# A two-layer encoder step on one core: weight sums formed in place one chunk a pair, casts ordered by edges, adds moved between two engines

## The chip, the cores and the metric

The kernel runs on one core of a Trainium2 chip. The metric is the device time of one execution in microseconds, the median of several runs. TensorE does the matrix products, VectorE, ScalarE and GpSimd the work between them, and SyncE's queue issues nearly all transfers between the chip's memory (HBM) and the on-chip buffers (SBUF). TensorE writes its sums to PSUM banks, from which VectorE and ScalarE fetch them. Each engine works through its own instructions in order: one that waits holds up all behind it.

## The reference, cut to what matters

Two layers on 1024 prompt frames and 64 sample frames (1088 columns, `T`), model width 1024:

```python
for layer in range(DEPTH):                       # DEPTH = 2
    if layer < N_A:                              # layer 0: state-space mixer
        mp, hp_new, cp_new = ssd_mixer(rmsnorm(xp, nw[0]), h0, c0, *params)
    else:                                        # layer 1: banded attention on a shared K/V
        ...
        mp = prompt_band_attention(qp, kp, vp, attn_rel_bias[i]) @ attn_w_o[i]
    xp = xp + rmsnorm(mp, nw[1])
    xp = xp + rmsnorm(swiglu(rmsnorm(xp, nw[2]), ffn_w_in[layer], ffn_w_out[layer]), nw[3])
    ...                                          # the same for the sample frames

def swiglu(u, w_in, w_out):
    g, up = jnp.split(u @ w_in, 2, axis=-1)
    return (jax.nn.silu(g) * up) @ w_out         # hidden width 2816
```

The change lies in the feed-forward part (`swiglu`) of both layers and in what follows it in layer 0: the second normalisation, the residual, and the operands of layer 1's first products. All data are 32-bit.

## The kernel before

**Products.** A 32-bit operand is split into a high part (ScalarE casts it) and a low part (VectorE subtracts the cast from the value), and a product of two such operands takes three matmuls: high x high, high x low, low x high. A tensor of the activations is held with the model width on the partitions; the 1088 columns are four quarters, `QS`: q = 0 and 1 of 256, q = 2 and 3 of 288. Column half b = 0 is quarters 0 and 1, b = 1 is quarters 2 and 3.

**Seven products in place of eight.** Both matrices of the feed-forward part are cut into 2 x 2 blocks, and seven block products P1 to P7 (`PRODS`, `SINGLE`) with sums of blocks before and after take the place of eight. So weights appear as plain parts `r0` and `b22` and as the two sums `ta` and `tb`, and the hidden activations as blocks `a11`, `a12`, `a21`, `a22` and sums `s1` to `s4`.

**First matrix, the pair loop.** `RUN` lists 22 positions. Position 0 is hidden tile pair 5 and position 1 pair 4 (b = 1 only), positions 2 to 17 are pairs 6 to 21 (both b), positions 18 to 21 are pairs 0 to 3 (b = 1 only). (Pairs 0 to 4 of b = 0 run before it without block sums, `plain_pairs`.) `run_pair` (L1454 on) issues a pair's products in order, P1 (b=0), P1 (b=1), P2 (b=0) and so on, 14 in a pair of both halves, each of 12 matmuls (L1485 to L1487), and after each its evacuation: a ScalarE copy (L1497) or VectorE adds (`add`, L1474) and, at the end, the hidden products (`times`, L1470). P6 and P7 go on adding into the bank that P1 filled, so they wait until ScalarE's copy has read it; P3 goes on in P5's bank, after VectorE's add has read it.

**Weights** (`Weights`, L234 on). `load` (L265) brings two tiles `raw` a pair; `pair` forms `ta` and `tb` (L323, L324, L341, L342; the first two on GpSimd, or on VectorE where the item has "dve"), and `part` (L369, L370) splits `b22`, `r0`, `ta`, `tb`. The three places for split weights (`hl`) are freed as the pair's products finish, r0's after P2, and refilled for the next pair. The cast of `b22` has a gate: GpSimd copies one column of `W.last`, the pair before's cast `ta`, into its output tile (L367), so that the cast can't start before that. All this is issued with priority `W.pri`, 3000 (`HIP`) within the loop; the evacuations have 3000 too. The planner that orders VectorE, ScalarE, GpSimd and the transfers takes among the ready instructions the one first in program order, with the priority counted as so many instructions earlier. TensorE's order is that of the program.

**Late work** (`hid.late`). After each product but the first P1 of a pair, one late step is issued (two where only b = 1 runs and more than four wait). Late steps are the block sums of the hidden activations (`form`, L1358: 4 for each b, after every second pair, and put ahead of others) and the chunks of the second matrix's weight sums (`chunk`, L1412). There are 16 chunks a layer, each of four sums `WT1` to `WT4` of four blocks, which `load` (L1399) brings from HBM and whose results go back to HBM (`wt`, L1413) for the second matrix. `side` queues them after a position's products: two chunks at positions 2, 8, 10, 12, 14 and 16 (with three empty steps between them), one at 9, 11, 13 and 15, none at 3 to 7; the first blocks are loaded at position 1, those of the third chunk at 7, and the others as soon as the chunk before is formed. A chunk uses five tiles of the ring `sg` (`SGB` = 5): its four blocks and `d`. The first sum of a chunk or a block group has a gate too, a one-column VectorE copy (L1406, L1353) from `hid.gate`, the last ScalarE evacuation.

**Operand loader.** After pair 21 `loader7` brings the blocks of the hidden activations from HBM (L1735) and `late_cast` splits them (L1704, L1705); within the loop a GpSimd copy of one column of `hid.gate` (L1702) is the gate.

**Second matrix** (`wino`, L1531 on; matmuls L1583 to L1585). `PHASES`: P1, P6, P2, P7, P5, then P4 (b=0), P4 (b=1), P3 (b=0), P3 (b=1). Each evacuation adds to the accumulators `p1`, `u2`, `u3`, `c22` (L1612), and `square` sums the squares for the normalisation (`add_sq`, L520 to L525: ScalarE squares, GpSimd or VectorE adds).

**Quarter ends of layer 0** (`EndU`). A quarter is finished after P4 (q = 0, then 2) or P3 (q = 1, then 3). `rb_steps` takes the sum of squares: matmuls with ones (L532), ten small VectorE steps (L538 to L549), a diagonal (L553), a matmul that spreads it (L561), a ScalarE copy (L567, L569). Then for each of 8 column blocks m: scale (L1835), add the residual (L1836, odd m on GpSimd but for q = 3), split for layer 1 (`split`, L1792 and L1793: one ScalarE cast and one VectorE subtraction for each m and each of one or two parts), square and sum again (`tail`, on GpSimd for q < 2 and odd m). The split operands `u` lie in cells of 384 columns, three to a tile (`u_slice`). Layer 1's first products (L498 to L500) need all m of a slice: slice 0 is quarter 0 and half of quarter 1.

## Time and profile before

| | |
|---|---|
| median of 3 runs | 3063.84 us (3063.11 to 3065.03) |
| profiled execution | 3065.48 us, of which the span from first to last instruction is 3063.8 us |
| mean granted TensorE clock | 0.984 |
| HBM read / written | 309.81 MB / 108.00 MB |
| pair loop, layer 0 / layer 1 | about 941 to 1375 us / about 2375 to 2800 us |
| second matrix, layer 0 / layer 1 | about 1375 to 1633 us / about 2800 to 3050 us |

The profile is one execution. Busy time of an engine is the sum of its instructions' time. A row of windows has, after the stretch and its length, the busy us (and number) of TensorE's matmuls, its weight loads, VectorE (DVE), ScalarE (ACT) and GpSimd (POOL), then the granted TensorE clock as a share of full speed, the share of the transfer engines and GB/s. A row of the timeline has start and duration in us, engine, line, operation, output and input, and in brackets how long the engine had stood idle before it and which instruction ended that. A row of groups has the busy time in us and the mean of one in ns, then the idle time before. A row of transfers has the KB of each and the us from issue to landing.

### The profile page before, as it was taken

The page shows a single profiled execution, that of the slowest core. Times are in us where ns is not written, and L with a number is a line of the kernel's source. Part 1 is how long each engine was busy: PE and PEld are TensorE (multiplying, and loading weights), DVE is VectorE, ACT ScalarE, POOL GpSimd, SP SyncE. Part 2 cuts the span into 40 slices and gives each one's busy share as a digit, 9 for nine tenths or more (in the row PEclk, how much of TensorE's full clock was granted, in tenths as well). Part 3 has the DMA queues.
Part 4 walks back from the last instruction along what each step waited for, and adds up shares of the span by engine and source line. Part 5 has one row for each costly group of instructions (what it writes and reads, how often), then busy time and mean ns, then how long its engine had stood idle before and what let it go on. Part 6 is the DMA issues. An engine that isn't in the chain of part 4 may idle for free. (4 is left out here: it accounts for less than half of the span.)

```text
span 3063.8 us, 60130 instructions
## 1 busy us (share of the span) xinstructions
PE 2934.7 (96%) x22295; PEld 2863.1 (93%) x22295; DVE 2317.7 (76%) x5263; ACT 1476.2 (48%) x2894; POOL 652.6 (21%) x870
## 2 busy tenths in 40 slices
PE   8999999999998999999987999999899999999998
PEld 8899999999998999999987899999899999999998
DVE  8988888885878667786687777777668776778567
ACT  6655556554534333345454555555543433235552
POOL 1334343421342212110033000000153221211011
PEclk9999999999999999999998999999999999999999
DMA  3333232335443445667765222112333344666665
GB/s 118 116 89 107 91 102 95 102 116 160 147 142 115 131 138 175 205 196 240 232 211 152 69 66 80 62 62 79 126 131 131 125 132 150 193 199 208 191 193 186
DMA packets 296535, 426.24 MB, mean 139 GB/s; under 512 B 31184, under 2 KB 250896, under 8 KB 296240
## 3 DMA queue, kind: packets, MB, share of 16 engines
q1 hardware_dynamic: 296176, 422.32, 43.8%
q8 instruction: 175, 2.87, 0.4%
q14 instruction: 120, 0.98, 0.1%
q0 software_dynamic: 64, 0.07, 0.0%
HBM read 309.81 MB, written 108.00 MB: 136 GB/s over the span
## 5 line engine op out<-in xcount | busy, mean ns | idle before, releaser
L498 PE MATMUL mm<-r,hl 128*128 128x384 f32 (+2 forms) x1632 | 550.8, 338 | 8.6 <-ACT r L2195 5.8
L499 PE MATMUL mm<-r,hl 128*128 128x384 f32 (+2 forms) x1632 | 531.9, 326 | 6.1 <-DVE r L1793 5.4
L500 PE MATMUL mm<-r,hl 128*128 128x384 f32 (+2 forms) x1632 | 531.7, 326 | 1.4 <-DVE hl L370 1.4
L1486 PE MATMUL px<-r,hl 128*128 128x288 f32 (+1 forms) x1192 | 350.5, 294 | 0.0
L370 DVE TENSOR_TENSOR hl<-raw,hl 128x1024 fp32r<-128x1024 f32 (+2 forms) x230 | 257.1, 1119 | 120.6 <-ACT hl L369 119.0
L498 PEld LDWEIGHTS mm<-r,hl 128*128 128x128 f32 x1632 | 312.7, 192 | 11.5 <-ACT r L2195 6.0
L499 PEld LDWEIGHTS mm<-r,hl 128*128 128x128 f32 x1632 | 312.6, 192 | 8.3 <-DVE r L1793 6.9
L1485 PE MATMUL px<-r,hl 128*128 128x288 f32 x1056 | 312.7, 296 | 7.7 <-ACT p L1497 4.7
L500 PEld LDWEIGHTS mm<-r,hl 128*128 128x128 f32 x1632 | 311.6, 191 | 2.0 <-DVE hl L370 2.0
L1487 PE MATMUL px<-r,hl 128*128 128x288 f32 x1056 | 311.4, 295 | 0.0
L369 ACT CAST hl<-raw 128x1024 fp32r<-128x1024 f32 (+2 forms) x230 | 216.8, 943 | 135.5 <-PE po L1585 44.1
L1485 PE MATMUL px<-rx,hl 128*128 128x256 f32 x816 | 231.0, 283 | 18.0 <-ACT p L1497 18.0
L525 POOL TENSOR_TENSOR ssum<-ssum,sq 128x288 f32<-128x288 f32 (+1 forms) x142 | 147.3, 1039 | 434.5 <-ACT sq L524 412.6
L1487 PE MATMUL px<-rx,hl 128*128 128x256 f32 x816 | 228.9, 281 | 0.0
L1486 PEld LDWEIGHTS px<-r,hl 128*128 128x128 f32 x1192 | 224.5, 188 | 0.1
L1485 PEld LDWEIGHTS px<-r,hl 128*128 128x128 f32 x1056 | 199.2, 189 | 9.4 <-ACT p L1497 5.7
L1487 PEld LDWEIGHTS px<-r,hl 128*128 128x128 f32 x1056 | 199.0, 188 | 0.0
L1486 PE MATMUL px<-rx,hl 128*128 128x256 f32 x680 | 191.0, 281 | 0.0
L1583 PE MATMUL po<-rx,hl 128*128 128x256 f32 (+1 forms) x650 | 189.3, 291 | 1.7 <-ACT p L1606 1.7
L1585 PE MATMUL po<-rx,hl 128*128 128x256 f32 (+1 forms) x650 | 188.6, 290 | 2.5 <-DVE hl L370 2.5
L1584 PE MATMUL po<-rx,hl 128*128 128x256 f32 (+1 forms) x650 | 188.0, 289 | 0.0
L1485 PEld LDWEIGHTS px<-rx,hl 128*128 128x128 f32 x816 | 155.2, 190 | 20.3 <-ACT p L1497 20.3
(424 smaller groups left out, 8566.6 us busy)
## 6 DMA issues: line engine op xcount, KB each, us to landing
raw<-in_w_f_dram SPq DMA_DIRECT2D x108, 512.0 KB, 3.8
sg<-hop SPq DMA_DIRECT2D x154, 144.0 KB, 3.2
sg<-hop SPq DMA_DIRECT2D x166, 128.0 KB, 3.1
raw<-in_w_in_dram SPq DMA_DIRECT2D x40, 512.0 KB, 3.4
sg<-in_w_f_dram SPq DMA_DIRECT2D x96, 192.0 KB, 3.4
wt<-sg SPq DMA_DIRECT2D x96, 192.0 KB, 2.5
raw<-in_w_so_dram SPq DMA_DIRECT2D x32, 512.0 KB, 3.8
dm<-acd SPq DMA_DIRECT2D x64, 192.0 KB, 3.6
```

Source lines behind the costliest of these rows:

```text
L369: self.nc.scalar.copy(h, v)
L370: (eng or self.eng or self.nc.vector).tensor_tensor(lo, v, h, op=ALU.subtract)
L498: PE.matmul(ps[:, :n], h_, xh, start=(first and i == 0), stop=False)
L499: PE.matmul(ps[:, :n], h_, xl, start=False, stop=False)
L500: PE.matmul(ps[:, :n], l_, xh, start=False, stop=(last and i == nk - 1))
L525: (eng or G).tensor_tensor(ssum[:, :n], ssum[:, :n], q[:, :n], op=ALU.add)
L1485: PE.matmul(ps, wh, ah[:, k, :], start=(k == 0 and not on), stop=False, skip_group_check=on)
L1486: PE.matmul(ps, wh, al[:, k, :], start=False, stop=False, skip_group_check=on)
L1487: PE.matmul(ps, wl, ah[:, k, :], start=False, stop=(k == 3), skip_group_check=on)
L1583: PE.matmul(ps[b][:, :n], wh, xh, start=(k == 0), stop=False)
L1584: PE.matmul(ps[b][:, :n], wh, xl, start=False, stop=False)
L1585: PE.matmul(ps[b][:, :n], wl, xh, start=False, stop=(k == KH - 1))
```

## The change

The edits, in the order of the diff:

- The gates go. In their place `tc.issue_after(ins)` adds an order edge without a wait: what is issued within the block comes behind `ins` on that engine's queue. `b22`'s cast is put behind the last weight cast (`W.last`, now any of them), late steps behind the last VectorE evacuation (`hid.dve`), loaded operands' casts behind `hid.act` and `hid.dve`.
- Chunks: loaded once at position 0 and then after every chunk; one is queued at each of positions 1 to 16. Its sums are written over blocks that are no longer needed, so `d` goes; three of its four tiles lie in a ring of their own, `sx`.
- Layer 0 alone: the weights' priority is 0 from position 0 to pair 20, 3000 again from pair 21.
- Wide copies: the cells of `u` are dealt so that three neighbouring m lie in one tile; `split` handles m = 0, 1, 2 in one cast and one subtraction at m = 2, and 4, 5, 6 at m = 6.
- Engines: layer 0's sums of squares in P3 go from GpSimd to VectorE; at the quarter ends the sums and residuals of q = 1 go to VectorE, the sums of q = 2 to GpSimd, those of q = 3 to VectorE.
- Quarter 3's end is begun 5.5 instead of 4.0 planned us after its last product.
- The tiles for layer 1's norms (`rba`) are allocated after layer 0's pair loop and freed after attention.

```diff
     def part(self, it, key, ring, v, eng=None, gate=None):
...
-        if gate is not None:
-            self.nc.gpsimd.tensor_copy(h[:, 0:1], gate[:, 0:1])
         with self.tc.high_priority(self.pri):
-            self.nc.scalar.copy(h, v)
+            with self.tc.issue_after(gate) if gate is not None else ExitStack():
+                self.last = self.nc.scalar.copy(h, v).ins
             (eng or self.eng or self.nc.vector).tensor_tensor(lo, v, h, op=ALU.subtract)
...
     def u_slice(s):
         n = SL[s][1]
-        ucells[s] = [UC.get() for _ in range(2 * KD)]
-        u[s] = [(rr(ucells[s][2 * k][0][:, :n]), rr(ucells[s][2 * k + 1][0][:, :n])) for k in range(KD)]
+        at, wide, alone = {}, [(h, m) for m in (0, 4) for h in range(2)], [(h, m) for m in (3, 7) for h in range(2)]
+        while wide or alone:
+            if wide and UC.left() in (0, 3):
+                h, m = wide.pop(0)
+                for k in range(3):
+                    at[h, m + k] = UC.get()
+                uw[s, h, m] = rr(at[h, m][1]["t"][:, :3 * 384]).rearrange("p (k n) -> p k n", k=3)
+            else:
+                h, m = alone.pop(0)
+                at[h, m] = UC.get()
...
-            if i in (1, 7):
+            if i == 0:
                 self.load()
-            elif self.todo and (i == 2 or 8 <= i < FT - 5):
-                self.late += [lambda gate, i=i: self.chunk(i, gate) for i in range(4)]
-                if i % 2 == 0:
-                    self.late += [lambda gate: None] * 3
-                    self.late += [lambda gate, i=i: self.chunk(i, gate) for i in range(4)]
+            elif self.todo:
+                self.late += [lambda i=i: self.chunk(i) for i in range(4)]
...
-            self.parts = [stage[0]()[:, :nk * P] for _ in range(4)]
+            self.parts = [(self.sx.tile([P, 384], F32, tag="sx", bufs=3, name="sx") if i else stage[0]())[:, :nk * P] for i in range(4)]
...
-                (WT3, d, b22, b12, ALU.subtract), (WT1, b22, b12, b11, ALU.subtract),
-                (WT2, b12, d, b11, ALU.add), (WT4, b11, b21, b12, ALU.subtract),
+                (WT3, b22, b22, b12, ALU.subtract), (WT1, b12, b12, b11, ALU.subtract),
+                (WT2, b11, b22, b11, ALU.add), (WT4, b21, b21, b11, ALU.subtract),
...
             for _ in range((len(hid.late) > 0) + (len(hid.late) > 4 and len(bs) == 1) if p_ != P1 or b == bs[-1] else 0):
-                hid.late.pop(0)(hid.gate)
+                with tc.issue_after(hid.dve):
+                    hid.late.pop(0)()
...
-                                square(2 * b + 1, at("u2"), n)
+                                square(2 * b + 1, at("u2"), n, None if layer else V)
...
-                    if phase[0] < 2 and left:
-                        G.tensor_copy(h_[:, 0:1], hid.gate[:, 0:1])
-                    with tc.high_priority(LDP):
+                    with tc.high_priority(LDP), ExitStack() as eg:
+                        if phase[0] < 2:
+                            for ins in (hid.act, hid.dve):
+                                eg.enter_context(tc.issue_after(ins))
                         A.copy(h_, t_)
                         V.tensor_tensor(l_, t_, h_, op=ALU.subtract)
...
                 def split(self, q, y, m, s, c, c0, c1):
-                    ym = y[m // 4][:, m % 4, c0:c1]
-                    uh, ul = (v[:, c:c + c1 - c0] for v in u[s][m])
+                    if m % 4 < 2:
+                        return
+                    if m % 4 == 2:
+                        ym = y[m // 4][:, :3, c0:c1]
+                        uh, ul = (uw[s, h, m - 2][:, :, c:c + c1 - c0] for h in range(2))
+                    else:
+                        ym = y[m // 4][:, 3, c0:c1]
+                        uh, ul = (v[:, c:c + c1 - c0] for v in u[s][m])
...
-                        yield 0, 4.0
+                        yield 0, 5.5
...
-                            add_sq(tot[m % len(tot)], y[m // 4][:, m % 4, :], n, m < len(tot), G if q < 2 or m % 2 else V, None if last else xs[m])
+                            add_sq(tot[m % len(tot)], y[m // 4][:, m % 4, :], n, m < len(tot), V if q % 2 else G, None if last else xs[m])
...
-                            (V if last or m % 2 == 0 else G).tensor_tensor(ym, ym, xs[m], op=ALU.add)
+                            (V if q % 2 or m % 2 == 0 else G).tensor_tensor(ym, ym, xs[m], op=ALU.add)
...
                     run_pair(t_, W.get(), bs, ends, ops, hid, px, tmp, i == 0)
+                    if not layer:
+                        W.pri = HIP if t_ == FT - 1 else 0 if t_ > 4 else W.pri
                     hid.side(i)
```

More of the change, by code (lines that the diff above doesn't have):

```diff
@@ L1347, in form, with one @@
             (a21, a11, a22, a12), n, q = x, BN[b] // 2, [None, None]
-            def one(i, gate):
+            def one(i):
                 if i < 2:
                     q[i] = nsb.tile([P, 384], F32, tag=("sq", "ssum")[i], bufs=2 + i, name="hs")[:, :n]
-                if i == 0 and gate is not None:
-                    V.tensor_copy(q[0][:, 0:1], gate[:, 0:1])
                 nm_, d, x_, y_, op = (
@@ L1365, in form @@
                 self.open.add(b)
-            self.groups.append([lambda gate, i=i: one(i, gate) for i in range(4)])
+            self.groups.append([lambda i=i: one(i) for i in range(4)])
         def order(self, bs):
@@ L1495, in run_pair @@
                 if p_ in (P1, P6, P7):
-                    hid.gate = t_new({P1: "p1", P6: "u2", P7: "u3"}[p_])
-                    A.copy(hid.gate, ps)
+                    hid.act = A.copy(t_new({P1: "p1", P6: "u2", P7: "u3"}[p_]), ps).ins
                 if p_ == P2:
@@ L1553, in square @@
                     G.memset(ss[q][0][:, n:], 0.0)
-            add_sq(ss[q][0], v, n, not ss[q][1])
+            add_sq(ss[q][0], v, n, not ss[q][1], eng)
             ss[q][1] += 1
@@ L1886, in back @@
                     r.put()
+                hid.sx = pool(e2, f"sx{layer}", side="right")
                 for i, (t_, bs) in enumerate(RUN):
@@ L1895, in back @@
                 while hid.late:
-                    hid.late.pop(0)(None)
+                    with tc.issue_after(hid.dve):
+                        hid.late.pop(0)()
                 hid.drop()
@@ L1902, in back @@
             if not layer:
+                rbp = pool(rbs, "rbp", side="right")
+                rba.extend(rbp.tile([P, 384], F32, tag=f"rbf{s}", name="rbf") for s in range(NSL))
                 st.spawn(prescale(), 20.0)
@@ L1925, in hybrid_kernel @@
     ffn_plan(0)
-    rbp = pool(ctx, "rbp", side="right")
-    rba = [rbp.tile([P, 384], F32, tag=f"rbf{s}", name="rbf") for s in range(NSL)]
+    rbs, rba = ExitStack(), []
     done2 = []
@@ L2272, in hybrid_kernel @@
         st.wait_for(lambda: cur["C"] == 8 * NCH)
+    rbs.close()
     yY = ExitStack()
```

23 lines of the change are left out of this document (8 added, 15 removed).

## The prediction, made before the change was run

> **What bounds the kernel now.** I read the page's busy shares first, then one table of stages, then the idle entries on TensorE's timeline, and for each long one what VectorE, ScalarE and GpSimd did just before it.
>
> ```profile
> PE 2934.7 (96%) x22295; PEld 2863.1 (93%) x22295; DVE 2317.7 (76%) x5263; ACT 1476.2 (48%) x2894; POOL 652.6 (21%) x870
> ```
>
> TensorE is busy for 96%, and the diff neither removes nor reorders a matmul: PRODS, SINGLE, PHASES and KORD stay. (The "other product order" of the description is not in it.) So the change can win only idle time of TensorE, 3063.8 - 2934.7 = 129 us, and time at a lowered clock. The stages that the diff touches, by windows (busy us of each engine, then granted clock, DMA share and GB/s):
>
> ```profile
> 940.00:1000.00 60.00, 52.35 (x389) 51.86 (x388) 50.53 (x68) 25.90 (x41) 13.14 (x10) 0.94 0.36 116
> 1000.00:1150.00 150.00, 150.00 (x1206) 150.00 (x1205) 98.60 (x183) 52.31 (x100) 31.32 (x29) 1.00 0.43 138
> 1150.00:1330.00 180.00, 175.15 (x1392) 173.72 (x1390) 134.39 (x248) 60.14 (x116) 31.80 (x30) 1.00 0.60 192
> 1330.00:1380.00 50.00, 47.72 (x359) 47.09 (x358) 46.27 (x96) 27.90 (x58) 8.39 (x21) 1.00 0.65 194
> ...
> 1560.00:1700.00 140.00, 114.41 (x698) 108.50 (x697) 112.31 (x269) 66.40 (x156) 46.16 (x55) 0.88 0.54 162
> 2370.00:2430.00 60.00, 53.30 (x409) 52.55 (x408) 50.45 (x68) 26.51 (x42) 14.48 (x11) 0.97 0.35 117
> ...
> 2600.00:2750.00 150.00, 145.03 (x1152) 143.66 (x1151) 113.85 (x204) 48.73 (x96) 26.93 (x25) 1.00 0.59 191
> 2750.00:2790.00 40.00, 34.95 (x262) 34.24 (x262) 33.48 (x69) 20.52 (x42) 8.39 (x21) 1.00 0.63 201
> ```
>
> TensorE is idle in them for 7.7, 0, 4.9, 2.3, 25.6, 6.7, 5.0 and 5.1 us, 57 us in all: the starts of the pair loop (940, 2370), its second half (1150, 2600), its column-half-1 pairs (1330, 2750), and the quarter ends with the head of attention (1560). Only from 1560 on is the clock low for long: 0.12 of 114 us is a further 13.7 us.
>
> **Chunks: the second half of the loop.** TensorE, then VectorE before the first of the two (start, duration, operation, idle before it and what ended that):
>
> ```profile
> 1194.76 0.40 PE L1485 MATMUL px<-r,half 128*128 128x288 f32 x1 [1.56 <-DVE c L1474]
> ...
> 1239.16 0.40 PE L1485 MATMUL px<-r,half 128*128 128x288 f32 x1 [1.31 <-DVE c L1474]
> ```
>
> ```profile
> 1182.84 0.15 DVE L1406 COPY sg<-p 128x1 f32<-128x1 f32 x1 [2.43 <-DMA wt<-sg]
> ...
> 1190.96 0.15 DVE L1406 COPY sg<-u 128x1 f32<-128x1 f32 x1 [2.83 <-DMA wt<-sg]
> 1193.18 1.15 DVE L1412 TENSOR_TENSOR sg<-sg 128x384 f32<-128x384 f32 x2 [2.07 <-DMA sg<-in_w_f_dram]
> 1194.25 0.45 DVE L1474 TENSOR_TENSOR c<-px,u 128x288 f32<-128x288 f32 x1
> ```
>
> The one-column gate copy needs a fifth staging buffer whose last contents are still being stored. Placed in order on VectorE, it stands for 2.43 and 2.83 us, the next chunk's sum for another 2.07, and the add that frees the bank for P3 (L1474) behind them is late. Over the whole run the gate line sat idle this often (us, times):
>
> ```profile
>   DMA wt<-sg: 42.0, 16
> ```
>
> The stall recurs 44 us later, after two pairs: only every second pair is fed two chunks. From 1000 to 1150 TensorE has no idle time: of seven pairs there two have two chunks, the first of them long loaded, and five have none. The change feeds one chunk to each of positions 2 to 17, forms it in place without a fifth tile, and drops 32 chunk gates. VectorE's 128 sums stay. The idle time at stake is 4.9 + 5.0 = 9.8 us. What is late next is the load of the following chunk:
>
> ```profile
> sg<-in_w_f_dram SPq DMA_DIRECT2D x96, 192.0 KB, 3.4
> wt<-sg SPq DMA_DIRECT2D x96, 192.0 KB, 2.5
> ```
>
> One of the three new slots is refilled after its store: a sum of 0.6 (1.15 for two above), 2.5 and 3.4 us, and I allow 0.8 for two issues: 7.3 us. In a pair that also has eight block sums the chunk is formed at products 10 to 13 of 14, in the next one at 2 to 5, so a slot has five products. A product is 12 matmuls at 150/1206 = 0.124 us, 1.5 us; five are 7.5 us. That is just in time. If half of the 16 such handovers (8 a layer) cost 0.5 us, 4 us come back; bounds 0 and 16 x 1 us. I take 8 gained and 4 given back.
>
> **Casts by order, weight priority.** Position 2 of layer 0, VectorE, ScalarE and TensorE:
>
> ```profile
> 985.82 1.77 DVE L341 TENSOR_TENSOR tt<-tt,raw 128x512 f32<-128x512 f32 x1 [1.20 <-POOL tt L323]
> 987.52 1.51 DVE L1470 TENSOR_TENSOR c<-p,u 128x288 f32<-128x288 f32 x1
> ```
>
> ```profile
> 989.12 0.37 ACT L1497 COPY p<-px 128x256 f32<-128x256 f32 x1 [3.96 <-DVE c L1470]
> ```
>
> ```profile
> 989.54 0.39 PE L1485 MATMUL px<-rx,hl 128*128 128x256 f32 x1 [3.33 <-ACT p L1497]
> ```
>
> A sum for a later pair's weights (L341) waits for GpSimd at the head of VectorE, and the product of the running pair (L1470) stands behind it; ScalarE's copy and P6 wait for that. After position 0 the change puts layer 0's weight work at priority 0, so that L1470 (priority 3000) goes first. The 3.33 us go, and with them the low clock that follows:
>
> ```profile
> 990.00:1000.00 10.00, 10.00 (x70) 10.00 (x69) 3.64 (x8) 2.83 (x6) 0.00 (x0) 0.83 0.44 158
> ```
>
> 0.17 of 10 us is 1.7, so 5.0 are at stake; I take 4.5 (bounds 0 and 5). The trace thus charges an idle of 3.33 us with a clock loss, while the 1.56 us above left it at 1.00. [...]
>
> Layer 1 keeps its priority, and its like stall (2420, in the window of 6.7 us) stays: 0. The earlier stall of layer 0, and what else was late there:
>
> ```profile
> 949.11 0.52 PE L1485 MATMUL px<-rx,hl 128*128 128x256 f32 x1 [4.32 <-ACT p L1497]
> ```
>
> ```profile
> 946.45 1.22 DVE L370 TENSOR_TENSOR hl<-tt,hl 128x1024 fp32r<-128x1024 f32 x1
> ```
>
> ScalarE stood behind a cast that waited for a transfer. The new order edge puts that cast behind the pair's last cast, but P6 reads operand parts that VectorE finishes at 946.45 + 1.22 = 947.67, so 1.4 of the 4.32 us can go. I take 1.
>
> The gates on GpSimd:
>
> ```profile
> L369 ACT CAST half<-raw 128x512 fp32r<-128x512 f32 x44 | 27.2, 618 | 80.4 <-POOL half L367 62.7 <-DMA raw<-in_w_f_dram 17.6
> L367 POOL CAST half<-hl 128x1 fp32r<-128x1 f32 x42 | 20.8, 495 | 143.9 <-PE px L1487 82.4 <-ACT hl L369 61.3
> ```
>
> These 42 gates of 0.5 us go, and the loader's like them (L1702). ScalarE is 48% busy, so most of its 62.7 us of waiting hid under the matmuls: nothing by itself, since the order they forced remains as an edge. In the half-1 pairs (2.3 + 5.1 = 7.4 us), where load casts and pair evacuations mix and the last two-chunk feed runs over, I take 2.5 (bounds -3 and 7.4). The four loads that move from position 1 to 0 meet weight loads, which cost up to 2 us there, or miss them: 0.
>
> **Quarter ends.** TensorE, then GpSimd:
>
> ```profile
> 1607.40 0.61 PE L532 MATMUL nst<-ones,ss 128*128 128x1 f32 x4 [0.49 <-POOL ss L525]
> ...
> 1622.71 2.04 PE L561 MATMUL nbp<-dg,frac 128*128 128x256 f32 x4 [5.54 <-DVE dg L553]
> ...
> 1642.75 0.69 PE L499 MATMUL mm<-r,hl 128*128 128x384 f32 x1 [3.86 <-DVE r L1793]
> ...
> 1648.99 1.01 PE L532 MATMUL nst<-ones,ssum 128*128 128x1 f32 x4 [2.92 <-POOL ssum L525]
> ```
>
> ```profile
> 1638.70 0.18 POOL L515 MEMSET ssum<- 128x96 f32 x1 [3.07 <-PE nst L532]
> ...
> 1647.41 1.52 POOL L525 TENSOR_TENSOR ssum<-ssum,sg 128x256 f32<-128x256 f32 x2 [4.14 <-ACT sg L524]
> ```
>
> Quarter 1's adds stand on GpSimd behind a memset that waits for TensorE; its residuals feed the operands for which TensorE waits 3.86 us, its sum the 2.92 us. The change puts its 4 residual adds and 7 sums on VectorE, and the 7 sums of P3's squares too; quarter 2's 3 VectorE sums go to GpSimd. Prices, on the one and on the other:
>
> ```profile
> 1605.46 0.45 DVE L525 TENSOR_TENSOR ssum<-ssum,sg 128x288 f32<-128x288 f32 x1
> ```
>
> ```profile
> L525 POOL TENSOR_TENSOR ss<-ss,sq 128x256 f32<-128x256 f32 (+1 forms) x7 | 8.1, 1163 | 13.0 <-ACT sq L524 12.9
> ```
>
> Quarter 1 costs VectorE 11 x 0.45 = 5.0 us at most, 4.1 if each overlaps the next by 0.08. What it wins back are conflicts with GpSimd; the same kind of small step takes
>
> ```profile
> 1612.50 0.15 DVE L547 TENSOR_TENSOR nv<-nv 128x2 f32<-128x2 f32 x1
> ...
> 1613.44 0.75 DVE L548 SCALAR_TENSOR_TENSOR nv<-nv 128x2 f32<-128x2 f32 x1
> ```
>
> the second while GpSimd has an operation. Each of the 11 operations that leave GpSimd can have cost VectorE such 0.6 us; if half did, 3.3 us come back and VectorE nearly breaks even. [...] Were the engines independent, the 4.1 us would lengthen quarter 1 and cancel the next two gains.
>
> Wide copies: three operations of 256 become one of 768, whose nearest rows on VectorE are
>
> ```profile
> L370 DVE TENSOR_TENSOR hl<-raw,hl 128x768 fp32r<-128x768 f32 x4 | 3.8, 948 | 0.8 <-ACT hl L369 0.8
> ...
> L1793 DVE TENSOR_TENSOR r<-c,r 128x256 fp32r<-128x256 f32 x6 | 2.5, 412 | 0.0
> ```
>
> 3 x 0.41 - 0.95 = 0.29 us a group at most, two to four groups a quarter, against which columns 0 and 1 wait for column 2. I take 0 (bounds -1 and 1). The sum of 2.92 goes whole: 2.9. Of the 3.86, 2 go, since VectorE stays full. Before the 5.54, VectorE is full:
>
> ```profile
> 1610.00:1620.00 10.00, 6.62 (x47) 5.97 (x45) 10.00 (x30) 4.69 (x10) 5.27 (x5) 1.00 0.70 213
> ```
>
> GpSimd has as many operations there as now (some squares less, three sums more), so only 1 goes. The 0.49 goes: 0.5. Of the 13.7 us of clock I take 3, for the two stalls near 1645; the one at 1622 still lowers it. Together 9.4. The later start (5.5 for 4.0) moves quarter 3's steps by 1.5 us behind matmuls: 0, at most 1.5 either way.
>
> **Sum.** 8 - 4 + 4.5 + 1 + 2.5 + 9.4 = 21.4 us. The profiled execution took 3065.5 us (span 3063.8 and 1.7 around it); 3065.5 - 21.4 = 3044.1. The median shown is 1.6 lower, so **3042 us**.
>
> **Rivals.** *All of it goes*: 9.8 without give-back, 5.0, 1.4, 7.4, and at the quarter ends 15 us of idle time and 9 of clock: 48 us, 3016. For it speaks that the stalls form a chain at 1616 to 1650; against it VectorE at 100% there. 3016 to 3030, chance 0.15. *The waits return*: the casts, loosed from their copies, and the just-in-time loads put others at the head of VectorE, and the quarter ends win only the 2.9: between 3050 and 3062, middle 3057. For it: 16 handovers without reserve. Chance 0.18. *Slower*: layer 0's weight casts at priority 0 fall behind the block and chunk sums. A cast of r0 has ten products, 15 us, from the release of its buffer to its use; VectorE has 134 of 180 us to do. It decides from where the cast's VectorE half (1.22 us) ends later than that; at 2 us in each of 16 pairs it costs 32, net +11: 3075. Against it: a quarter of VectorE is free. Chance 0.12.
>
> **How the numbers follow.** Forecast 0.55 (3030 to 3054). A measurement tells about 0.2%, 6 us, from no change. Faster (below 3057.7): 0.55 + 0.15 + 0.08 of the second rival, 0.78; same: its other 0.10 and 0.02 of the third, 0.12; slower: 0.10. The range leaves out half of the first rival and nearly all of the slower one: 3020 to 3066.
>
> **What would show it.** No VectorE wait for wt stores and no idle time in 1150 to 1330; no 3 us before P6 at 989; the sum at 1649 on VectorE without idle time before it, the clock near 1 from 1643; the stall at 1622 still there. The forecast is wrong if the pair loop of layer 0 has new idle time before products that read cast weights, or if quarter 1's operands end later than 1645 counted from the same matmul.

## The result and the profile after

| | before | after |
|---|---|---|
| median of the runs compared, us | 3063.48 (3060.27 to 3075.25, 6 runs) | 3043.05 (3036.29 to 3044.18, 6 runs) |
| ratio, with its 95% interval | | 0.9924 (0.9906 to 0.9942) |
| profiled execution, us (span) | 3065.48 (3063.8) | 3044.18 (3042.5) |

The medians lie 20.4 us apart, 0.67%; the ratio of the runs says 0.76%, and its interval leaves out 1. The forecast was 3042. The total agrees almost exactly; the terms do not, as the stages show, so the agreement is luck. One execution of one kernel (e4, the profiled one) ran at a mean clock of 0.607 for 4337.81 us and is left out of every figure. The page's line of the engines, and the windows (busy us of each engine, then clock, DMA share, GB/s). The second halves of the two pair loops are the rows of 1150 and 2590; layer 1 runs some 10 to 21 us earlier than before, so its windows start 10 earlier:

```profile
PE 2930.9 (96%) x22295; PEld 2863.9 (94%) x22295; DVE 2303.7 (76%) x5183; ACT 1480.1 (49%) x2870; POOL 608.8 (20%) x774
```

```profile
940.00:1000.00 60.00, 53.16 (x409) 52.72 (x409) 53.30 (x72) 27.87 (x44) 11.02 (x8) 0.97 0.41 130
1000.00:1150.00 150.00, 150.00 (x1206) 150.00 (x1205) 107.14 (x184) 52.90 (x102) 30.45 (x22) 1.00 0.56 177
1150.00:1330.00 180.00, 180.00 (x1441) 180.00 (x1440) 129.46 (x231) 65.84 (x129) 27.79 (x20) 1.00 0.53 165
1330.00:1380.00 50.00, 49.09 (x377) 48.76 (x376) 42.53 (x86) 28.13 (x57) 0.18 (x1) 1.00 0.66 194
1560.00:1700.00 140.00, 117.06 (x710) 112.16 (x709) 114.14 (x279) 65.33 (x141) 27.83 (x35) 0.89 0.49 154
2360.00:2420.00 60.00, 53.91 (x399) 52.79 (x398) 50.40 (x70) 26.67 (x42) 9.48 (x7) 0.94 0.41 133
2590.00:2740.00 150.00, 150.00 (x1205) 150.00 (x1204) 106.64 (x184) 53.00 (x101) 25.52 (x19) 1.00 0.51 166
2740.00:2780.00 40.00, 38.25 (x284) 37.62 (x283) 36.86 (x73) 23.28 (x47) 0.00 (x0) 1.00 0.58 174
```

Read the second number: TensorE is busy for 180.00 of 180 and 150.00 of 150 us in the second halves of both loops, where it was idle for 4.9 and 5.0. The start of the loop (940, 2360) and the quarter ends (1560) still have 6.8, 6.1 and 22.9 us of idle time.

Windows at fixed times blur once one kernel runs ahead. All 22295 matmuls come in the same order in both traces but for the few of the norms at the quarter ends, so the k-th matmul of one can be set against the k-th of the other. The table gives what each stage gained on the profiled execution of before, by the starts of the matmuls at its edges (us; stages by before's time; minus is a loss). "Half-1 pairs" are those of which only b = 1 runs. The columns e1 to e12 are the experiments below; e4 is the kernel of e9.

```
                        after  e1    e2    e3    e5    e6    e7    e8    e9    e10   e11   e12
0-940                   -1.0   1.0   0.6  -1.3   2.4  -0.3  -1.2  -2.9  -0.6  -0.1   0.8   0.7
940-1000  loop, start    2.5   0.6   2.3   3.1   2.0   0.8   2.1   3.8   3.3   2.9   2.6   2.5
1000-1150                0.0   0.0   0.0   0.0   0.0   0.0   0.0  -0.3   0.0   0.0   0.0   0.0
1150-1330 2nd half       7.2   0.1   5.7   7.2   7.2   7.2   7.2   7.2   7.2   7.2   7.2   7.2
1330-1395 half-1 pairs   1.9   0.7  -0.1   1.2   0.0   1.2  -3.1   0.9   1.3   1.7   1.5  -0.7
1395-1540                0.1   0.1   0.2   0.1   0.1   0.1   0.1   0.1   0.1   0.1   0.1   0.1
1540-1800 quarter ends   5.1   6.1   5.3   8.4   1.6   5.1   3.9   4.1   6.0   5.4   9.1   4.6
1800-2370 attention     -4.1  -0.6  -3.7  -3.1  -1.4  -0.8  -1.0  -5.9  -0.6  -3.7   0.0  -0.5
2370-2430 loop, start   -1.2  -1.5   0.1  -0.2   0.0  -1.4  -2.8   5.8  -1.3   5.5   0.0   0.2
2430-2600                0.0   0.0   0.0   0.0   0.0   0.0   0.0  -1.6   0.0  -0.6   0.0   0.0
2600-2750 2nd half       6.7  -0.1   3.1   6.7   6.7   6.7   6.7   6.6   6.7   6.7   6.7   6.7
2750-2795 half-1 pairs   3.6  -1.3  -0.5   4.1   4.5   4.7   1.1   4.4   4.8   4.3   4.7   2.0
2795-end                 0.6  -0.6  -1.6   0.1  -0.9  -1.2   0.0   0.7  -0.5  -0.6  -3.9   0.7
all                     21.3   4.5  11.4  26.2  22.1  22.1  13.0  23.0  26.3  28.8  28.9  23.4
```

The chunk stages with the half-1 pairs behind them hold 19.4 of the 21.3 us; the prediction had 6.5 for them. The quarter ends give 5.1, not 9.4, and the start of layer 0's loop 2.5, not 5.5. Two kinds of row must be told apart. The rows of 1000, 1150, 1395, 2430 and 2600 are the same to 0.1 us in every kernel whose edit does not touch them. All others move between kernels that have the same code there: 0-940, attention and the end by several us, the loop starts and the half-1 pairs by 1 to 2.

### The profile page after: what moved, and what is told of

Its sections match the earlier page's. It is cut to its first block, busy times and chain, and to the rows that moved or that the text cites. A ratio compares the mean times of both kernels' runs of the same rounds, so it can differ in the third digit from the quotient of the medians.

```text
span 3042.5 us, 59836 instructions
## 1 busy us (share of the span) xinstructions
PE 2930.9 (96%) x22295; PEld 2863.9 (94%) x22295; DVE 2303.7 (76%) x5183; ACT 1480.1 (49%) x2870; POOL 608.8 (20%) x774
```

## The experiments

Each ratio is to the kernel before, run on the same chip. Beside the five sets of runs that kernel had medians of 3063.5 to 3069.2 us, so compare the ratios rather than the times. Only e1's interval lies apart from that of the kernel after (0.9906 to 0.9942); all others overlap it, those of e7 and e12 at its upper end. What the other experiments show, they show by their traces. Line numbers in a fence are those of the kernel that it shows.

**e1: the chunk part undone.**

```diff
-            if i == 0:
+            if i in (1, 7):
...
-            elif self.todo:
+            elif self.todo and (i == 2 or 8 <= i < FT - 5):
...
+                self.d = stage[0]()[:, :nk * P]
+                if self.gate is not None:
+                    V.tensor_copy(self.d[:, 0:1], self.gate[:, 0:1])
...
-                (WT3, b22, b22, b12, ALU.subtract), (WT1, b12, b12, b11, ALU.subtract),
+                (WT3, d, b22, b12, ALU.subtract), (WT1, b22, b12, b11, ALU.subtract),
```

> The kernel after, with the chunk part alone as it was: two chunks in every second pair from position 8, a fifth staging tile, a gate copy for each chunk. Theory: nearly all the time won in the two pair loops hangs on this part. Against the kernel before, the same matmuls gained 6.6 us in 1150 to 1300 and 6.7 us in 2600 to 2750, and the column-half-1 pairs behind them 2.6 and 4.0 us more. With the old chunks 13 to 20 us come back: 3057 to 3064 us, ratio to before 0.996 to 1.000, and in 1150 to 1330 TensorE again has some 5 us of idle time, with VectorE standing on a gate of a chunk behind a store of wt. Rival: the new order of the casts and layer 0's priority give half of it; then 3050 us, and the idle time in layer 0's 1150 to 1330 is under 2.5 us.

Measured: 3060.04 us, ratio 0.9972 (0.9960 to 0.9984). Windows, then groups of VectorE's gate line (us busy, mean ns of one, then idle time ahead and what ended it), of this kernel:

```profile
1150.00:1330.00 180.00, 174.54 (x1386) 173.11 (x1386) 132.51 (x243) 59.72 (x117) 29.78 (x20) 1.00 0.62 193
2600.00:2750.00 150.00, 145.01 (x1152) 143.68 (x1151) 108.53 (x195) 49.19 (x95) 23.00 (x18) 1.00 0.63 196
```

```profile
L1412 DVE COPY sg<-u 128x1 f32<-128x1 f32 x20 | 3.0, 148 | 19.8 <-DMA wt<-sg 19.8
...
L1412 DVE COPY sg<-p 128x1 f32<-128x1 f32 x12 | 1.8, 154 | 17.6 <-DMA wt<-sg 17.6
```

The idle time of 5.5 and 5.0 us is back, and so are 37.4 us in which VectorE stands on a one-column copy behind a store of wt. The stages lose 7.1 and 6.8 us against the kernel after, the half-1 pairs 1.2 and 4.9: 20.0 us in the traces, 14.7 by the ratios, both in the theory's range; the rival's 3050 is out. No other edit matters in the second halves of the loops: with all of them in place these stages gain 0.1 and -0.1 us.

**e2: in place and without gates, but in the old rhythm.**

```diff
-            elif self.todo:
-                self.late += [lambda i=i: self.chunk(i) for i in range(4)]
+            elif self.todo and (i == 2 or 8 <= i < FT - 5):
+                self.late += [lambda i=i: self.chunk(i) for i in range(4)]
+                if i % 2 == 0:
+                    self.late += [lambda: None] * 3
+                    self.late += [lambda i=i: self.chunk(i) for i in range(4)]
```

> The kernel after, with the chunks formed in place in the new tiles and without gates, but fed in the old rhythm (two in every second pair from position 8). It tells the two halves of the chunk part apart. Theory: the stall of before came from the fifth tile, whose gate copy waited for a store at the head of VectorE's queue; in place nothing waits for a store on VectorE except through a reload, so the rhythm costs little: 3043 to 3048 us, ratio 0.992 to 0.995. Rival: the burst itself is the cause, since the second chunk of a pair is loaded into tiles whose stores have only just been issued (the 7.3 us of the prediction); then VectorE waits for the loads of sg and sx in every second pair, and 1 to 1.5 us come back in each of 10 pairs with two chunks: 3053 to 3058 us.

Measured: 3052.15 us, ratio 0.9938 (0.9919 to 0.9956). The time is just under the rival's range and the ratio within the theory's, so neither came as it stood. VectorE, then TensorE, of this kernel in layer 1:

```profile
2651.75 0.42 DVE L1475 TENSOR_TENSOR c<-px,u 128x256 f32<-128x256 f32 x1
2656.79 0.56 DVE L1413 TENSOR_TENSOR sg<-sg,sx 128x384 f32<-128x384 f32 x1 [4.62 <-DMA sx<-in_w_f_dram]
2657.26 0.45 DVE L1475 TENSOR_TENSOR c<-px,u 128x288 f32<-128x288 f32 x1
```

```profile
2657.77 0.41 PE L1486 MATMUL px<-r,half 128*128 128x288 f32 x1 [1.25 <-DVE c L1475]
```

The next chunk's first sum waits 4.62 us for a load at the head of VectorE's queue; the add that frees TensorE's bank (L1475) stands behind it. It is before's stall with a load in place of a store. So neither half of the chunk part does it alone. In place without the fifth tile keeps 5.7 + 3.1 of the 7.2 + 6.7 us of the two loop stages; the rhythm of one a pair brings the other 1.5 and 3.6, and 2.0 and 4.1 in the half-1 pairs.

**e3 and e5: the quarter ends' engines undone; in e5 the wide copies too.** The edit of e3 (that of the copies stands at e4):

```diff
-                                square(2 * b + 1, at("u2"), n, None if layer else V)
+                                square(2 * b + 1, at("u2"), n)
...
-                            add_sq(tot[m % len(tot)], y[m // 4][:, m % 4, :], n, m < len(tot), V if q % 2 else G, None if last else xs[m])
+                            add_sq(tot[m % len(tot)], y[m // 4][:, m % 4, :], n, m < len(tot), G if q < 2 or m % 2 else V, None if last else xs[m])
...
-                            (V if q % 2 or m % 2 == 0 else G).tensor_tensor(ym, ym, xs[m], op=ALU.add)
+                            (V if last or m % 2 == 0 else G).tensor_tensor(ym, ym, xs[m], op=ALU.add)
...
-                        yield 0, 5.5
+                        yield 0, 4.0
```

> The kernel after, with the engines of the quarter ends as before (quarter 1's residual adds and sums of squares and P3's sums of squares on GpSimd, quarter 2's half on VectorE) and the later start (5.5) back at 4.0; the wide copies stay. The prediction has 9.4 us for the quarter ends; the same matmuls stand only 5.0 us better after this stage than before it, and 3.9 us of all that was won go again in attention. Theory: the moves are worth 5 us: 3046 to 3050 us, ratio 0.993 to 0.996, with the 2.9 us before the sum of squares of quarter 1 (GpSimd ssum) back. Rival: they are worth the predicted 9.4 us and the wide copies eat the rest: 3052 us or more, ratio 0.996 or more. Second rival: the stage gives back in attention whatever it wins, so nothing changes: 3043 us.

> The kernel after with the quarter ends wholly as before: engines, start at 4.0, and copies of one column block. From 1540 to 1800 the same matmuls gained 5.1 us in the kernel after and 8.4 us with its engines as before and the copies wide. Theory: the wide copies win 8 us there and the engine moves lose 3 of them, so here the stage gains nothing: 8 us more than with wide copies alone, 3046 to 3050 us, ratio 0.992 to 0.995. Rival: the stage gains from what is changed ahead of it (no gates on GpSimd, no backlog of chunks from the pairs), and neither edit of the ends is worth anything: 3038 to 3042 us, with 6 to 8 us gained in 1540 to 1800 all the same.

Measured: e3 3039.54 us, 0.9900 (0.9884 to 0.9916); e5 3045.17 us, 0.9930 (0.9906 to 0.9954). Undoing the engine moves cost nothing: all three expectations of e3 lie above what came. The time of e5 is just under its theory's range and the ratio within it, but that theory (copies win 8, moves lose 3) falls with e9, and e10, which has the quarter ends of e3 and gains 5.4 there for 8.4, shows why not to build on one trace.

**e4 and e9: the copies narrow, the engine moves kept.** `u_slice` is as in the kernel before, and in `split`:

```diff
-                    if m % 4 < 2:
-                        return
-                    if m % 4 == 2:
...
+                    ym = y[m // 4][:, m % 4, c0:c1]
+                    uh, ul = (v[:, c:c + c1 - c0] for v in u[s][m])
```

> The kernel after, with the operand copies of the quarter ends one column block at a time as before; the engine moves stay. The prediction has 0 with bounds of 1 us either way. Theory: the wide copies cost: TensorE waits 4.8 us at 1631 for a cast of three columns (ScalarE, from the split) where before it waited 1.6 us for one, so the narrow copies win 1 to 3 us: 3040 to 3042 us. Rival: they are what unloads VectorE there; without them 2 to 4 us come back: 3045 to 3047 us. Prediction: within 1 us of the kernel after, 3042 to 3044 us.

> The kernel after with copies of one column block, as in the earlier run of it, for its trace. Of the four corners of the quarter ends three have one now: 1540 to 1800 gained 8.4 us with wide copies alone, 5.1 us with both edits, 1.6 us with neither. Theory: with the engine moves alone the gain is between neither and both, 2 to 5 us, since their part (less waiting for GpSimd's sums) and the copies' part both shorten the same chain and don't add up. Rival: the moves cost the same 3.3 us with narrow copies, so they alone lose: 1.7 us worse than before.

Measured: e4 3043.72 us, 0.9917 (0.9901 to 0.9934), as the prediction said. e9 is the same kernel once more, for its trace: 3039.14 us, one run. The quarter ends gained 6.0 us, above the theory's 2 to 5 and far from the rival's loss: no sign that the moves lose, or that they do worse with narrow copies than with wide ones.

**e11: quarter 1's residual adds shared with GpSimd again**, its sums still on VectorE.

```diff
-                            (V if q % 2 or m % 2 == 0 else G).tensor_tensor(ym, ym, xs[m], op=ALU.add)
+                            (V if last or m % 2 == 0 else G).tensor_tensor(ym, ym, xs[m], op=ALU.add)
```

> The kernel after with one line back: quarter 1's residual adds alternate between GpSimd and VectorE again; sums of squares stay on VectorE. Theory: the residuals feed the casts that the products wait for, and on one engine these eight steps stand behind one another with VectorE's sums between them (the 4.8 us wait at 1631 for a cast that had waited for a residual); with the line back most of the 3.3 us that the engine moves cost is won: 7 to 8.4 us gained in 1540 to 1800, 3039 to 3042 us. Rival: it is the sums that are in the way, then the stage stays at 5 us, 3043 us or more.

Measured: 3040.43 us, 0.9921 (0.9901 to 0.9941), in the theory's range, with 9.1 us in the stage. But the wait that was to be shortened grew, from 4.78 us to 6.70, so the theory is not borne out. Five variants (e1, e2, e6, e7, e8) share the quarter ends of the kernel after and gain 3.9 to 6.1 there; e3 and e10 share theirs and gain 8.4 and 5.4; e5 and e12 have those of before and gain 1.6 and 4.6. A single execution thus moves this stage by 2 to 3 us. The edits of the quarter ends are worth some 2 to 3 us together (a mean of 4.9 in those five and the kernel after, less 3.1 in e5 and e12, or 2.1 with before's own 0 among them), no more than that spread.

The traces say what moves the stage. Its matmuls are the same in all kernels, so its length is idle time of TensorE, what a lowered clock costs, and a rest of 210 to 213 us. In the traces of before and after the granted clock is 1.00 or 0.50 throughout; the second row counts half of the busy time at 0.50 as lost. (In the pair loops of these two, matmuls of 256 columns start every 0.117 us at 1.00 and every 0.213 at 0.50, those of 288 every 0.133 and 0.240, medians.)

```
us of 1540-1800      before after  e1    e2    e3    e5    e6    e7    e8    e9    e10   e11   e12
TensorE idle          33.7  30.9  30.8  32.2  29.0  32.7  30.8  28.9  31.5  28.6  29.2  32.1  31.9
lost at half clock    14.5  12.3  10.2   9.6  11.5  13.8  11.7  16.1  11.3  12.7  15.0   6.8  11.5
```

e11's 9.1 us are clock: it is idle for longer than the kernel after. e3 and e10 differ by 0.2 us in idle time and by 3.5 in clock. By idle time alone, the ends of before stand at 31.9 to 33.7 us, those of the kernel after at 28.9 to 32.2, the wide copies without the engine moves (e3, e10) at 29.0 and 29.2, the moves without the copies (e9) at 28.6. So each half does as well alone as both together; which of them brings the gain stays open.

**e6: the priority of layer 0's weight work undone.**

```diff
-                    if not layer:
-                        W.pri = HIP if t_ == FT - 1 else 0 if t_ > 4 else W.pri
```

> The kernel after without the edit that puts layer 0's weight work at priority 0 from position 1 on. The prediction has 4.5 us for it. Theory: nothing; in the kernel after the sum for a later pair's weights still stands ahead of the product that P6 waits for, and TensorE still waits 3.38 us at 989, because the order on VectorE follows what the planner takes to be ready first, and not priority alone. 3042 to 3045 us, and layer 0's pair loop within 1 us of the kernel after. Rival: without it sums of later pairs stand ahead of running ones from position 4 on, and 2 to 4 us of the gain in 1150 to 1330 go: 3046 to 3048 us.

Measured: 3044.84 us, 0.9933 (0.9911 to 0.9955). Nothing is lost in 1150 to 1330; at the start of the loop 1.7 us. The stalls of positions 0 and 2 of layer 0 in the kernel after, TensorE, then VectorE before the second:

```profile
949.26 0.39 PE L1480 MATMUL px<-rx,hl 128*128 128x256 f32 x1 [3.46 <-ACT p L1491]
...
989.65 0.38 PE L1480 MATMUL px<-rx,hl 128*128 128x256 f32 x1 [3.38 <-ACT p L1491]
```

```profile
985.91 1.77 DVE L341 TENSOR_TENSOR tt<-tt,raw 128x512 f32<-128x512 f32 x1 [1.79 <-POOL tt L323]
987.61 1.53 DVE L1465 TENSOR_TENSOR c<-p,u 128x288 f32<-128x288 f32 x1
```

The sum L341 is still first and P6 still waits 3.38 us (3.33 before). The order of the two is the same with the edit and without. The two operations also take long here, 1.77 and 1.53 us, while GpSimd works beside them; in e8 they took 0.68 and 0.46 while GpSimd stood still, so some 2 of the 3.38 us are their length. What the kernel after does win at this place is clock. Before, after, and e6 (TensorE's clock is the third number from the right), the 5 us behind the stalls at 949 and 989:

```profile
950.00:955.00 5.00, 5.00 (x35) 5.00 (x34) 4.77 (x9) 2.22 (x4) 0.00 (x0) 0.74 0.30 105
990.00:995.00 5.00, 5.00 (x30) 5.00 (x29) 3.22 (x7) 2.45 (x5) 0.00 (x0) 0.66 0.72 254
```

```profile
950.00:955.00 5.00, 5.00 (x31) 5.00 (x31) 5.00 (x9) 1.93 (x4) 0.00 (x0) 0.66 0.36 122
990.00:995.00 5.00, 5.00 (x43) 5.00 (x42) 4.68 (x10) 2.37 (x5) 0.00 (x0) 1.00 0.77 251
```

```profile
950.00:955.00 5.00, 5.00 (x35) 5.00 (x34) 5.00 (x9) 2.59 (x4) 0.00 (x0) 0.74 0.29 105
990.00:995.00 5.00, 5.00 (x30) 5.00 (x29) 4.10 (x8) 2.26 (x5) 0.00 (x0) 0.66 0.85 250
```

An idle of 3.33 us was followed by a clock of 0.66 before, one of 3.38 us by 1.00 after. 0.34 of 5 us is 1.7 us by the clock; by the starts of the matmuls before falls 1.5 us behind the kernel after in these 5 us, and e6 loses 1.7 in this stage. The edit does not decide it: e12 lacks it too and keeps 1.00 behind the second stall, e1 and e5 have it and fall to 0.66. Nor does the length of the idle time: the shorter of these two lost clock, the longer none.

What differs is where the stall falls. In the traces of before and after the 35 changes of the clock in each lie at multiples of 3.413 us from one another, to 5 ns, and the grid that they form lies 1.13 us later in the kernel after, counted from the start of the span. The stretches of that grid around the second stall, before, then after (the first number behind the length is TensorE's busy time):

```profile
986.75:990.16 3.41, 0.62 (x5) 0.62 (x6) 3.38 (x6) 0.37 (x1) 1.97 (x2) 1.00 0.13 34
990.16:993.57 3.41, 3.41 (x18) 3.41 (x17) 3.06 (x7) 2.05 (x4) 0.00 (x0) 0.50 0.82 293
```

```profile
984.46:987.88 3.42, 1.80 (x14) 1.57 (x13) 1.97 (x2) 0.91 (x2) 3.32 (x3) 1.00 0.30 100
987.88:991.29 3.41, 1.64 (x13) 1.64 (x14) 3.41 (x7) 1.19 (x3) 0.94 (x1) 1.00 0.43 147
991.29:994.70 3.41, 3.41 (x30) 3.41 (x29) 3.34 (x6) 1.55 (x4) 0.00 (x0) 1.00 0.66 210
```

Before, TensorE was idle for 2.79 us of one stretch, and the clock was 0.50 in the next. In the kernel after the stall is divided, 1.62 us in one stretch and 1.77 us in the next, and the clock stays at 1.00. In the pair loops of these two traces each of the five stretches at full clock with 2.35 us or more of idle time was followed by one at 0.50, and none with 1.77 us or less was. Outside the loops that division does not hold: before's stretch from 1635.28 has 0.65 us of idle time and the next is at 0.50. The length of a stall alone, by which the prediction told 3.33 us from 1.56, does not fit these rows.

**e7: the gate copies of the casts back, in place of the order edges.**

```diff
+        if gate is not None:
+            self.nc.gpsimd.tensor_copy(h[:, 0:1], gate[:, 0:1])
...
+                    if phase[0] < 2 and left:
+                        G.tensor_copy(h_[:, 0:1], hid.gate[:, 0:1])
```

> The kernel after with the one-column gate copies on GpSimd for the half casts and the loader's casts, in place of the order edges. Theory: order is the same, so 0 to 2 us: 3042 to 3045 us, with the losses, if any, in the column-half-1 pairs (1330 to 1395 and 2750 to 2795, where the loader casts run) and at the start of the loop. Rival: the gates stand in GpSimd's queue in front of sums for weights, and part of what the old chunks seemed to cost is theirs: 3047 to 3052 us.

Measured: 3052.61 us, 0.9948 (0.9930 to 0.9965). That is about the rival's time, but not by its reason: the second halves of the loops keep their 7.2 and 6.7 us. The loss is in the half-1 pairs, 5.0 and 2.5 us against the kernel after, and 1.6 at the start of layer 1's loop. In these pairs e7 and e12, the two with the gate copies, gain -3.1 and -0.7 us in layer 0 and 1.1 and 2.0 in layer 1; the kernel after and the seven others with edges and one chunk a pair gain 0.0 to 1.9 and 3.6 to 4.8. TensorE, ScalarE and VectorE of this kernel in layer 0's half-1 pairs:

```profile
1338.18 0.40 PE L1483 MATMUL px<-r,hl 128*128 128x288 f32 x1 [2.70 <-DVE u L1472]
```

```profile
1334.87 0.62 ACT L369 CAST half<-raw 128x512 fp32r<-128x512 f32 x1 [2.12 <-DMA raw<-in_w_f_dram]
1335.51 0.40 ACT L1495 COPY u<-px 128x288 f32<-128x288 f32 x1
```

```profile
1334.89 0.69 DVE L323 TENSOR_TENSOR tt<-raw 128x512 f32<-128x512 f32 x1 [1.38 <-DMA raw<-in_w_f_dram]
...
1337.67 0.82 DVE L1472 TENSOR_TENSOR u<-px,u 128x288 f32<-128x288 f32 x2
```

A weight transfer lands at 1334.8. On ScalarE its cast, on VectorE four operations on it and one of the loader's stand ahead of the add that TensorE needs (the first of the two L1472). In the kernel after that add is the second of the two at 1329.86, ahead of the transfer, and TensorE does not wait for it; one product earlier it waits 0.92 us, for a ScalarE copy. VectorE of the kernel after:

```profile
1329.86 0.81 DVE L1469 TENSOR_TENSOR u<-px,u 128x288 f32<-128x288 f32 x2
...
1333.27 0.69 DVE L323 TENSOR_TENSOR tt<-raw 128x512 f32<-128x512 f32 x1 [1.87 <-DMA raw<-in_w_f_dram]
```

**e8 and e10: an order edge on the weight sums too**, in e10 with the quarter ends' engines of before.

```diff
-            with self.tc.high_priority(self.pri):
+            with self.tc.high_priority(self.pri), (self.tc.issue_after(self.hid.dve) if self.hid is not None and getattr(self.hid, 'dve', None) is not None else ExitStack()):
                 v(ta[:, :512], ta[:, 512:], b11, op=ALU.add)
```

> The kernel after, and in addition the two sums of a pair's weights on VectorE get an order edge behind the last operation issued for the running pair, as the casts have it. It does what the prediction expected of the priority. Theory: TensorE's waits before P6 in position 2 (3.4 us in layer 0, 4.0 us in layer 1, and about 1.7 us of low clock behind each) go: 4 to 9 us, 3034 to 3039 us. Rival: the sums come too late in their turn, since the casts of ta and tb and the release of the raw buffers stand behind them; the wait moves to the products that read these casts: 3042 us or more.

> The kernel after with the order edge on the two weight sums and the quarter ends' engines and start as before (wide copies kept): the two variants that came out better than the kernel after, together. If they add: 7.0 us in layer 1 (2370 to 2430), less 1.6 us that came back in 2430 to 2600, some 1.4 us in layer 0 (940 to 1000), and 3.3 us at the quarter ends, 10 us in all: 3031 to 3036 us, ratio 0.987 to 0.990. Rival: the order edge's gain was noise of stages that the change doesn't touch, and the quarter ends give no more than alone: 3038 to 3042 us.

Measured: e8 3037.47 us, 0.9906 (0.9881 to 0.9931); e10 3036.03 us, 0.9902 (0.9887 to 0.9918), the one in its theory's range, the other at the end of its. In layer 1 the edge does what the prediction expected of the priority: the wait of 3.95 us becomes 0.44, and 2370 to 2430 gains 7.0 us on the kernel after, of which 2430 to 2600 gives 1.6 back. In layer 0 P6 still waits 2.15 us. ScalarE and VectorE of e8 there:

```profile
988.85 0.62 ACT L366 CAST half<-raw 128x512 fp32r<-128x512 f32 x1 [4.32 <-DMA raw<-in_w_f_dram]
989.38 0.67 ACT L1491 COPY p<-px 128x288 f32<-128x288 f32 x2
```

```profile
985.59 0.46 DVE L1465 TENSOR_TENSOR c<-p,u 128x288 f32<-128x288 f32 x1
```

The product (L1465) is now done at 986.05, but ScalarE's copies stand behind a cast that waits 4.32 us for a weight transfer. That transfer is issued at 985.20, behind two other loads of SyncE's queue, where the kernel after issues it at 980.96. So the sum is no longer in front, and in layer 0 the wait has moved, as e8's rival had it, though to a copy and not to a cast of ta or tb. e10 has the lowest median of all runs; the intervals of both overlap that of the kernel after, so neither is shown to be faster.

**e12: the chunk part alone on the kernel before**, with the other edits undone but for the move of the `rba` tiles. Against the kernel before:

```diff
-            if i in (1, 7):
+            if i == 0:
                 self.load()
-            elif self.todo and (i == 2 or 8 <= i < FT - 5):
...
+            elif self.todo:
+                self.late += [lambda i=i: self.chunk(i) for i in range(4)]
...
+            self.parts = [(self.sx.tile([P, 384], F32, tag="sx", bufs=3, name="sx") if i else stage[0]())[:, :nk * P] for i in range(4)]
...
+                    with tc.issue_after(hid.dve):
+                        hid.late.pop(0)()
```

> The chunk part alone on the kernel before: in place, one chunk a pair, new tiles, chunk and block sums held by order; every other edit (casts by order, priority, engines and start of the quarter ends, wide copies) as before. Theory, from the runs that took parts away: 7.2 us in 1150 to 1330 and 6.7 us in 2600 to 2750 as in the kernel after, the column-half-1 pairs no better than with the gate copies (3.1 us lost in layer 0, 1.1 us won in layer 1), the quarter ends within 2 us of before: about 12 us less than before, 3052 to 3056 us, ratio 0.995 to 0.997. Rival: the chunk part needs the others to show (its backlog meets the gates), and less than 8 us are won: 3058 us or more.

Measured: 3049.49 us, 0.9949 (0.9936 to 0.9963): 15.9 us of the change's 20.4 by the medians, 0.51 of its 0.76% by the ratios, just better than the range expected. The second halves of the loops gain 7.2 and 6.7, to the tenth what they gain in the kernel after, and the half-1 pairs -0.7 and 2.0. So the chunk part does not need the other edits, and it is two thirds or more of the change.

## Why the prediction came out right, and which of its steps did not

**Chunks: mechanism right, size wrong twice.** The net term was 4 us; the two stages gave 7.2 + 6.7 = 13.9. First, the stake of 9.8, of which 8 was counted, was read off the idle time, and the stalls cost more than that: in layer 1's stage six stalls show 5.0 us and cost 6.7, 0.28 more each. Second, the 4 us of give-back did not come. The handovers are late on VectorE, as forecast:

```profile
L1407 DVE TENSOR_TENSOR sx<-sx 128x384 f32<-128x384 f32 (+1 forms) x64 | 40.0, 624 | 16.9 <-issue 12.6 <-DMA sx<-in_w_f_dram 2.6 <-DVE sx L1407 0.6
...
L1407 DVE TENSOR_TENSOR sg<-sg,sx 128x384 f32<-128x384 f32 (+1 forms) x32 | 16.5, 517 | 11.5 <-DMA sx<-in_w_f_dram 11.5
```

28 us of waiting (16.9 + 11.5) in the kernel after; the 12.6 called issue are four waits of 3.0 to 3.3 us that end, like most others, as a load of `sx` lands (1140.24 for the sum at 1140.32). And TensorE has no idle time in either window, so with one chunk a pair each wait ended before TensorE needed the next add. The forecast took every late handover to reach TensorE.

**Half-1 pairs: 5.5 (1.9 + 3.6) for 2.5.** Right in kind. Either cause undone loses it: 1.2 and 4.9 in e1, 5.0 and 2.5 in e7. The parts do not add up, since both feed the same queues.

**Casts by order: costed at nothing, and that failed.** "ScalarE is 48% busy, so most of its waiting hid under the matmuls: nothing by itself" is the step. Without the edges the half-1 pairs lose 7.5 us, more than the 5.5 that they had gained, and e7's trace is 8.3 us longer. The order was taken to stay the same; in e7 it does not. Why the planner then puts sums that carry no edge ahead of an add is not shown. The 1 us that was forecast for the edges at 949 came: 4.32 us of idle time became 3.46, and with the gates back it is 4.32 (e7) and 3.82 (e12).

**Priority: 4.5 predicted, nothing shown.** The step "L1470 goes first" (L1465 in the kernel after) failed: the sum stays in front at either priority (e6). The likely reason is that the planner took the sum to be ready first and weighs priorities only among ready ones; what it took to be ready is not on record. An order edge does move the sum (e8). The 2.5 us won in this stage are 0.9 at 949 and a clock of 1.00 that the stall at 989 happened to keep.

**Quarter ends: 9.4 predicted, 5.1 in the trace, 2 to 3 by the runs.** The waits of the kernel after:

```profile
1612.79 2.05 PE L558 MATMUL nbp<-dg,frac 128*128 128x256 f32 x4 [5.89 <-DVE dg L550]
...
1631.34 0.69 PE L495 MATMUL mm<-r,hl 128*128 128x384 f32 x1 [4.78 <-ACT r L1794]
...
1664.18 0.69 PE L495 MATMUL mm<-r,hl 128*128 128x384 f32 x1 [2.98 <-DVE vt L2053]
```

The 2.92 before quarter 1's sum went, as forecast, and the stall at 1622 stayed (5.54, now 5.89, where 1 us was to go). But 3.86 at one product became 4.78 at an earlier one, and 2.98 us now stand ahead of a later one. With narrow copies (e9) the 4.78 is 1.92. Of the 9.4 forecast 6.4 were idle time and 3 clock; the trace has 2.8 (33.7 to 30.9) and 2.2 (14.5 to 12.3), so the step that failed is the waits for the operands: they moved and did not go. That the engine moves cost VectorE little was right, and the next rows show it, though the two windows do not hold quite the same operations: from 1600 to 1640 VectorE has 101 operations in 31.16 us in the kernel after, and 93 in 34.28 us in e3, where GpSimd is busy 19.08 us instead of 6.05. First after, then e3:

```profile
1600.00:1640.00 40.00, 27.40 (x145) 24.77 (x146) 31.16 (x101) 17.05 (x38) 6.05 (x9) 0.78 0.60 191
```

```profile
1600.00:1640.00 40.00, 26.93 (x143) 25.12 (x142) 34.28 (x93) 16.30 (x38) 19.08 (x21) 0.79 0.59 185
```

Over all of 1540-1800 it is 524 operations in 201.5 us, and 508 in 203.7 in e3. VectorE got cheaper, and TensorE had its operands no sooner: in this stage VectorE's time was not the whole chain.

**The sum.** 21.4 forecast, 21.3 in the trace, because 13 us too little at the chunks and half-1 pairs met 7 too much at the priority and the quarter ends and some 5 lost where 0 stood (attention and the start of layer 1's loop). That these nearly cancel is luck: the terms were wrong by some 13 us each way. Attention's 4.1 is put down to no edit by any run: in the other eleven traces it is 0.0 to 5.9. But all twelve kernels with edits are idle there for 32.4 to 35.3 us, and before's one trace for 31.1. Whether a loss of a few us belongs to what they share, the move of the `rba` tiles among it, or to that one trace, is open, since the move was never undone.

## What to carry to other kernels

Price a stall from the start of one matmul to the start of the next, and compare kernels by the k-th matmul where the order is the same: the rows that repeat to 0.1 us then show what an edit did, and those that move by 3 us cannot be read from one execution. Split such a row into idle time and time at a lowered clock before you credit an edit with it. Look for what stands at the head of an in-order queue and waits for a transfer: here a smaller priority did not move it (P6 waited 3.33 us before and 3.38 after), an order edge did (3.95 to 0.44 us in layer 1), and the next such instruction, on another engine, came into view. Spread just-in-time work evenly: the same loads that stalled TensorE in bursts of two (3.9 us idle in 2600 to 2750 of e2) cost it nothing at one a pair.

## What the hardware showed that was not expected

The six stalls in the second half of layer 1's loop before cost TensorE about 0.28 us each more than the idle time shown before them (5.0 us shown, 6.7 lost). Some 0.16 of it lies ahead: the matmul before the stall is shown as 0.28 to 0.30 us long, where the next would have started 0.12 to 0.13 us after its start. Some 0.10 lies behind: the second matmul after the stall starts 0.22 to 0.24 us after the first, in place of 0.12 to 0.14.

And of two stalls of nearly the same length, 3.33 and 3.38 us, one was followed by a clock of 0.50, which cost 1.5 us by the starts of the matmuls, and the other by none of it. The first lay with 2.79 us of its idle time in one stretch of the 3.413 us grid on which the clock changed in these two traces, the other with 1.62 and 1.77 us in two.
